# Down products of the first feed-forward chunks moved two units earlier and halved, one PSUM bank changed, residual additions given priority

## Chip, cores and metric

The kernel runs on one NeuronCore of a Trainium2 chip. The metric is the device time of one execution in microseconds (us): the median of three runs, 1444.62 us before the change (1444.34 to 1444.73). The engines are TensorE (PE, with its weight loads shown as PEld), VectorE (DVE), ScalarE (ACT), GpSimd (POOL) and SyncE (SP, which issues most DMAs).

## The reference

A decoder trunk of two layers works on 512 tokens of 1024 channels, in float32. Layer 0 has a mixer of a gated linear recurrence and pooling, layer 1 a Conformer convolution module. In both, a cross-attention into 256 memory tokens follows, and then the part that matters here, a gated MLP with a short convolution on its gate:

```
def conv_ffn(x, norm, w_up, dw_w, dw_b, w_down):
    h = rms_norm(x, norm) @ w_up                       # 1024 -> 2 * 3072
    g = causal_dwconv(h[..., :D_FF], dw_w, dw_b)       # width 3
    u = h[..., D_FF:]
    return (jax.nn.gelu(g) * u) @ w_down               # 3072 -> 1024
...
x = x + conv_ffn(...)                                  # at the end of each layer
```

## The kernel before

Channels lie on the 128 partitions and tokens along the free dimension; the residual is eight tiles `X[0]` to `X[7]` of 128 x 512. A float32 product is made of three matmuls (`mm3`, lines 186 to 188): every operand is split into a rounded high part (an ACT copy) and the rest, its low part (a DVE subtraction); high by high, high by low and low by high are added in PSUM.

**The feed-forward part** (`ffn`, once for each layer) has 24 chunks of 128 hidden channels, 0 to 23. Chunks 0 and 1, the plain pairs, are made in `opening()` with plain products. Chunks 2 to 23 are made by `unit(c)`, one after the other. A unit treats gate and value weights and the two halves of the tokens as a 2 x 2 block product with seven block products in place of eight. They are called, in the order of PE: s1 (into bank H), s2 (into F), a12 (into G), s3 (into F), then a11 of the next unit (`ahead`, into the next G), then s4 (into H) and a22 (into F). H is one half of the single bank of the pool `stat`; G and F come from the pool of five `mm` banks. In units 2 and 3 (`first` and `second`) a block product is twelve matmuls of 256 columns; from unit 4 on a product into G or F joins high and low part in one pass (line 791, eight matmuls: four of 512 columns and four of 256), and that into H stays twelve of 256.

**The weights of a unit** are four blocks, loaded by SP into `raw` (two blocks) and `wa` (two). The sums of blocks that the seven products need are made by DMAs that add in place, issued by POOL (lines 843, 846, 848), each after the split of the block that the addition overwrites. Each of the seven blocks is split by ACT (line 833) and DVE (line 840). The split of s1 and s2 for unit c+1 stands near the end of unit c.

**The gating of chunk c** begins at the end of unit c: DVE adds H and a copy of F (`add`, line 171), multiplies by the norm's scale, and then the convolution, the GeLU (line 918), the product with the value half (line 945) and the split of the result `ys[c]` (ACT line 948, DVE line 950) follow in small steps within unit c+1 (`next(left)`).

**The down products** of a group of four chunks are spread over the four units after it: unit c, for c from 4 on, takes 24 matmuls of 512 columns for two of the eight residual tiles (`Down`), into the two `aux` banks. In unit 4 (`seeded` is false) the banks start empty and DVE adds them to `X` (line 884). In later units ACT copies two `X` tiles into the banks first (`bank`, line 873) and copies them back after (`home`, line 878). The weights, 512 KB for each unit, come by one DMA into a `big` tile and are split by ACT (line 200) and DVE (line 203), one unit ahead; units 2 and 3 have no down products. The last group's products stand after the last unit; in layer 0 eight residual additions follow there (`sum`, line 884), each with `nxt.feed`: a square on ACT (line 251) and its addition on DVE (line 253). Their total gives the scale of the next norm (`norm.scale()`: line 319, then 355), and that the first product of the Conformer module. The weights of that module are split at the same time (line 167) with a priority of 100 instructions ahead (`AHEAD`).

**Order.** Within `opening` and the units the order of PE, ACT, DVE and POOL is the order of the program (`manual_schedule`); each of them takes its instructions strictly in that order. Outside, a scheduler orders them by priority; `high_priority(n)` moves an instruction n places ahead.

## Time and profile before

| | |
|---|---|
| median of three runs | 1444.62 us (1444.34 to 1444.73) |
| the profiled execution's own time | 1442.98 us |
| its span in the trace | 1441.2 us |
| busy PE, DVE, ACT, POOL | 1421.0, 1131.2, 939.2, 317.1 us |
| mean granted TensorE clock | 0.995 of full speed |

The views used are: the page of the whole profile; the waits, as a row "who waited <- for whom: us in total, times, longest"; the windows, one row for each stretch of time with the busy time of PE, PEld, DVE, ACT and POOL (instructions begun in brackets), the granted clock, the DMA engines' share and GB/s; the chain of waits, which is the work that ended last in order of time (start, us, what); and the timeline (start, us, engine, line, operation, out<-in, shape, count, and in square brackets the idle time before it and what ended it). Names such as `stat`, `mm`, `aux`, `raw` are tiles of the program. A matmul's duration in the timeline overlaps that of the next one, so what a block of matmuls takes is read from start to start. Units are counted from the start of their s1: in layer 0 unit 2 starts at 381.42, unit 3 at 391.50, unit 4 at 404.94 and unit 5 at 422.11 us of the span; in layer 1 at 1075.15, 1085.23, 1099.51 and 1117.57 us.

### The profile page before, as it was taken

Reading aid. Unit: us, or ns where it says so; the run is one execution under the profiler, and the core shown is the slowest. Engines: PE = TensorE matmul, PEld = TensorE weight load, DVE = VectorE, ACT = ScalarE, POOL = GpSimd, SP = SyncE. Lnnn points to the kernel's source line nnn. Section 1 sums busy time; section 2 is a strip of 40 time slices with the busy share of each in tenths; the row PEclk is TensorE's granted clock in tenths of the full one; section 3 lists DMA queues with packets and bytes.
Section 4 is the critical chain, followed back from the end, with each engine's and each line's share of the span. In section 5 each row is a group of like instructions: output and inputs, shape, how many; then the busy total and the mean of one; then the engine's idle time right before and its main releaser. Section 6 shows DMA issues by size and latency. Waiting matters only on the chain.

```text
span 1441.2 us, 22110 instructions
## 1 busy us (share of the span) xinstructions
PE 1421.0 (99%) x8142; PEld 1239.8 (86%) x8142; DVE 1131.2 (78%) x1908; ACT 939.2 (65%) x1704; POOL 317.1 (22%) x333
## 2 busy tenths in 40 slices
PE   9999999999999999999999999999998999999998
PEld 8888888988988888888878777899898888888887
DVE  6987776779777777777788997978787777777776
ACT  7568755667556676666665547767755676676664
POOL 0012300100112222122008992010002222222211
PEclk9999999999999999999999999999999999999999
DMA  8522232544477777776432354345337777777741
GB/s 304 190 87 90 88 131 68 124 109 139 100 173 174 165 178 169 165 183 161 142 117 88 118 165 142 110 85 135 110 96 176 166 172 175 167 174 171 174 127 59
DMA packets 80029, 204.28 MB, mean 142 GB/s; under 512 B 9008, under 2 KB 9520, under 8 KB 79920
## 3 DMA queue, kind: packets, MB, share of 16 engines
q1 hardware_dynamic: 50832, 150.15, 31.9%
q0 software_dynamic: 28800, 52.44, 21.2%
q8 instruction: 64, 1.05, 0.3%
q14 instruction: 45, 0.37, 0.1%
q10 hardware_dynamic: 288, 0.27, 0.1%
HBM read 145.16 MB, written 2.10 MB: 102 GB/s over the span
## 4 chain that ended last, share of the span: by engine, by line
PE 88%; DVE 4%; ACT 2%; POOL 2%; DMA 2%; issue 2%; SPq 0%; POOLq 0%; ACTq 0%; DVEq 0%
PE mm L791 19%; PE mm L187 12%; PE mm L186 12%; PE mm L188 12%; PE aux L186 7%; PE aux L187 7%; PE aux L188 7%; PE stat L186 3%; PE stat L188 3%; PE stat L187 3%; PE mm L463 2%; DMA raw<-wa 1%; DMA raw<-in_wv 1%; POOL actf L1550 1%; PE aux L538 0%
## 5 line engine op out<-in xcount | busy, mean ns | idle before, releaser
L186 PE MATMUL mm<-act,whi 128*128 128x512 f32 (+2 forms) x837 | 295.2, 354 | 1.7 <-ACT act L279 1.5
L187 PE MATMUL mm<-act,whi 128*128 128x512 f32 (+2 forms) x837 | 296.3, 354 | 0.3 <-DVE act L181 0.2
L188 PE MATMUL mm<-act,wlo 128*128 128x512 f32 (+2 forms) x837 | 295.8, 353 | 0.0
L791 PE MATMUL mm<-bigr,bigr 128*128 128x512 f32 x960 | 190.0, 341 | 0.0
L186 PEld LDWEIGHTS mm<-act,whi 128*128 128x128 f32 x837 | 158.1, 189 | 24.2 <-ACT act L279 2.0
L187 PEld LDWEIGHTS mm<-act,whi 128*128 128x128 f32 x837 | 158.5, 189 | 22.9 <-DVE act L167 1.0
L188 PEld LDWEIGHTS mm<-act,wlo 128*128 128x128 f32 x837 | 158.5, 189 | 21.0 <-DVE wlo L167 0.6
L840 DVE TENSOR_TENSOR bigr<-raw,bigr 128x512 fp32r<-128x512 f32 x176 | 121.0, 688 | 59.8 <-ACT bigr L833 56.0
L791 PEld LDWEIGHTS mm<-bigr,bigr 128*128 128x128 f32 x960 | 149.2, 190 | 18.3
L833 ACT ACTIVATE bigr<-raw 128x512 fp32r<-128x512 f32 x176 | 109.4, 624 | 75.8 <-DVE wlo L203 70.2
L846 POOL DMA_DIRECT2D raw<-wa x100 | 87.3, 893 | 310.7 <-DVE bigr L840 210.8
L186 PE MATMUL aux<-act,whi 128*128 128x512 f32 x399 | 155.6, 390 | 0.0
L187 PE MATMUL aux<-act,whi 128*128 128x512 f32 x399 | 155.5, 390 | 0.0
L188 PE MATMUL aux<-act,wlo 128*128 128x512 f32 x399 | 155.3, 389 | 0.0
L166 ACT ACTIVATE whi<-raw 128x1024 fp32r<-128x1024 f32 (+1 forms) x95 | 96.6, 1021 | 80.4 <-PE mm L187 44.4
L843 POOL DMA_DIRECT2D raw<-raw x50 | 43.3, 866 | 364.6 <-DVE wlo L840 281.1
L171 DVE TENSOR_TENSOR tmp<-mm,tmp 128x256 f32<-128x256 f32 x202 | 80.7, 418 | 51.7 <-ACT tmp L923 50.4
L791 PE MATMUL mm<-act,whi 128*128 128x512 f32 x320 | 119.4, 396 | 0.0
L923 ACT ACTIVATE tmp<-mm 128x256 f32<-128x256 f32 x160 | 55.5, 372 | 81.4 <-PE mm L791 81.4
L167 DVE TENSOR_TENSOR wlo<-raw,whi 128x1024 fp32r<-128x1024 f32 (+1 forms) x75 | 90.4, 1210 | 17.4 <-ACT whi L166 17.1
L188 PEld LDWEIGHTS aux<-act,wlo 128*128 128x128 f32 x399 | 74.9, 188 | 16.0
L187 PEld LDWEIGHTS aux<-act,whi 128*128 128x128 f32 x399 | 74.9, 188 | 15.9
(377 smaller groups left out, 3453.1 us busy)
## 6 DMA issues: line engine op xcount, KB each, us to landing
raw<-wa POOLq DMA_DIRECT2D x150, 256.0 KB, 3.4
wa<-in_wpair SPq DMA_DIRECT2D x88, 256.0 KB, 3.8
raw<-in_wpair SPq DMA_DIRECT2D x44, 512.0 KB, 3.7
big<-in_wdown SPq DMA_DIRECT2D x42, 512.0 KB, 4.5
raw<-raw POOLq DMA_DIRECT2D x50, 256.0 KB, 4.0
raw<-in_pw SPq DMA_DIRECT2D x24, 512.0 KB, 3.3
raw<-in_win SPq DMA_DIRECT2D x20, 512.0 KB, 3.3
raw<-in_wk SPq DMA_DIRECT2D x16, 512.0 KB, 3.3
```

What stands on the lines that cost most here:

```text
L166: A.activation(hi, src, AF.Copy)
L167: fetched[1] = (eng or V).tensor_tensor(lo, src, hi.bitcast(F32), op=ALU.subtract)
L171: V.tensor_tensor(out, a, b, op=ALU.add)
L186: PE.matmul(ps, wh, xh, start=first, stop=False, skip_group_check=onto)
L187: PE.matmul(ps, wh, xl, start=False, stop=False, skip_group_check=onto)
L188: return PE.matmul(ps, wl, xh, start=False, stop=last, skip_group_check=onto)
L791: PE.matmul(to, part, by, start=first and c == 0 and i == 0, stop=c == 3 and i == 1, skip_group_check=True)
L833: A.activation(self.w[name][0], self.block(name), AF.Copy)
L840: V.tensor_tensor(lo, self.block(name), hi.bitcast(F32), op=ALU.subtract)
L843: G.dma_start(self.r, self.z, accum_op=ALU.add)
L846: G.dma_start(block, self.a22, accum_op=ALU.add)
L923: A.activation(out, ps[:, M:], AF.Copy)
```

## The change

Four things are changed, the first three in both layers.

- The down products of chunks 0 to 3 no longer stand as 24 matmuls in each of the units 4 to 7. They are cut by chunk: chunks 0 and 1 go to units 2 and 3, two jobs of twelve matmuls in each (one job is two residual tiles), and chunks 2 and 3 to units 4 to 7, one job of twelve in each. The first job of a unit stands where the down products stood, behind s3; the second one stands between s4 and a22, and its copies home behind a22.
- The weights for that come as `Halves`: two DMAs of 256 KB into one `big` tile, which serves two jobs. They are loaded and split for unit 2 (split within unit 2), unit 3 (at the end of unit 2), units 4 and 5 together (at the end of unit 3) and units 6 and 7 together (in unit 5). From unit 8 on all is as before.
- H of units 2 and 3 is an `mm` bank in place of the `stat` bank.
- The eight residual additions at the end of layer 0's feed-forward part, with their squares, get the priority `URGENT` (600 places).

```
--- before.py
+++ after.py
@@ -856,15 +856,13 @@
         class Down:
 
 
-            def __init__(self, g, j):
-                self.g, self.j = g, j
-
-            def load(self):
-                self.w = Piece(I["wdown"][(layer * NG + self.g) * (C // 2) + self.j], big_f())
-
-            def products(self, i, ps, seeded=False, ks=range(GC)):
-                for k in ks:
-                    self.last = mm3(ps, blk(self.w, k * 2 * P + i * P), ys[self.g * GC + k], k == 0 and not seeded, k == GC - 1, seeded)
+            def __init__(self, g, j, ks, at=0):
+                self.g, self.j, self.ks, self.at = g, j, ks, at
+
+            def products(self, i, ps, seeded=False, ks=None):
+                for k in self.ks if ks is None else ks:
+                    at = self.at + (k - self.ks[0]) * 2 * P + i * P
+                    self.last = mm3(ps, blk(self.w, at), ys[k], k == self.ks[0] and not seeded, k == self.ks[-1], seeded)
 
             def bank(self, i, seeded):
 
@@ -885,7 +883,41 @@
                 if self.g == NG - 1:
                     nxt.feed(n)
 
-        downs = {c: Down(*divmod(c - GC, GC)) for c in range(GC, CF + GC)}
+        class Halves(Piece):
+
+
+            def __init__(self, js, half):
+                self.raw = big_f()
+                for i, j in enumerate(js):
+                    src = I["wdown"][layer * NG * (C // 2) + j]
+                    nc.sync.dma_start(self.raw[:, i * T : (i + 1) * T], src[:, half * T : (half + 1) * T])
+
+        group = [list(range(g * GC, (g + 1) * GC)) for g in range(NG)]
+        old, new = group[0][:2], group[0][2:]
+        downs = {c: [Down(*divmod(c - GC, GC), group[c // GC - 1])] for c in range(2 * GC, CF + GC)}
+        halves = {}
+        for i, c in enumerate((PLAIN, PLAIN + 1)):
+            downs[c] = [Down(0, 2 * i + k, old, k * T) for k in range(2)]
+            halves[c] = (2 * i, 2 * i + 1), 0
+            for k in range(2):
+                downs[GC + 2 * i + k] = [Down(0, 2 * i + k, new, k * T)]
+            halves[GC + 2 * i] = (2 * i, 2 * i + 1), 1
+        for c in (GC + 1, GC + 3):
+            halves[c] = None
+
+        def fetch_down(c):
+
+            if c <= CF and halves.get(c, 0) is not None:
+                d = downs[c][0]
+                w = Halves(*halves[c]) if c in halves else Piece(I["wdown"][(layer * NG + d.g) * (C // 2) + d.j], big_f())
+                for d in downs[c] + (downs[c + 1] if halves.get(c + 1, 0) is None else []):
+                    d.w = w
+
+        def split_down(c):
+            if c <= CF and halves.get(c, 0) is not None:
+                downs[c][0].w.high()
+                downs[c][0].w.low()
+
         done = set()
 
         def high(c, name):
@@ -970,8 +1002,26 @@
 
             nonlocal left, chains
             G, F = chains
-            down, seeded = downs.get(c), c > GC
-            H = stat_ps()[:, :M]
+            jobs = iter(downs[c])
+            H = main_ps()[:, :M] if c <= second else stat_ps()[:, :M]
+
+            def seeds():
+                nonlocal down, d, seeded
+                down, seeded = next(jobs, None), seeded is not None or c > first
+                if down:
+                    d = [down.bank(i, seeded) for i in range(2)]
+
+            def products():
+                if down:
+                    for ks in (down.ks[:-1], down.ks[-1:]):
+                        for i in range(2):
+                            down.products(i, d[i], seeded, ks)
+
+            def home(i):
+                if down:
+                    down.home(i, d[i], seeded)
+
+            down, d, seeded = None, None, None
             m(c, H, "s1", seven.T1)
             if c <= second:
                 high(c + 1, "s3")
@@ -987,8 +1037,9 @@
                 A.activation(u[:, :M], F, AF.Copy)
             if c == first:
                 both(c + 2, "a11")
-            if down:
-                d = [down.bank(i, seeded) for i in range(2)]
+                split_down(c)
+                fetch_down(c + 1)
+            seeds()
             next(left, None)
             both(c + 1, "s3")
             next(left, None)
@@ -1020,36 +1071,37 @@
             both(c + 2, "a11")
             high(c + 1, "a12")
             low(c + 1, "a12")
-            if down:
-                for ks in (range(GC - 1), (GC - 1,)):
-                    for i in range(2):
-                        down.products(i, d[i], seeded, ks)
+            products()
             if c + 3 in pairs:
                 pairs[c + 3].load()
             if c + 2 in pairs and c > first:
                 pairs[c + 2].load_second()
-            if c > second and c + 1 in downs:
-                downs[c + 1].w.high()
-                downs[c + 1].w.low()
-            if c + 2 in downs and first < c <= CF - 2:
-                downs[c + 2].load()
+            if c > second:
+                split_down(c + 1)
+                fetch_down(c + 2)
             high(c + 1, "s1")
             low(c + 1, "s1")
             high(c + 1, "s2")
             low(c + 1, "s2")
-            if c == second:
-                downs[c + 1].w.high()
-                downs[c + 1].w.low()
-            if down:
-                down.home(0, d[0], seeded)
+            if c <= second:
+                split_down(c + 1)
+                fetch_down(c + 2)
+            home(0)
 
             if c + 1 in pairs:
                 chains = ahead(c + 1)
-            if down:
-                down.home(1, d[1], seeded)
+            home(1)
+            more = len(downs[c]) > 1
+            if more:
+                seeds()
 
             m(c, H, "s4", seven.B22, False)
+            if more:
+                products()
             m(c, F, "a22", seven.T4, False)
+            if more:
+                home(0)
+                home(1)
             left = gating(c, g, f, u, F, H)
             next(left)
 
@@ -1107,7 +1159,7 @@
             w[-1].low()
             pairs[second + 1].load()
             pairs[second + 1].load_second()
-            downs[GC].load()
+            fetch_down(first)
             t = seven.sums(3, lambda: (next(g), next(g)))
             next(t)
             next(g, None)
@@ -1158,17 +1210,18 @@
             parked = []
             for n in range(PARKED):
                 if n + 1 < C // 2:
-                    downs[CF + n + 1].w = load_w(I["wdown"][(layer * NG + NG - 1) * (C // 2) + n + 1])
+                    downs[CF + n + 1][0].w = load_w(I["wdown"][(layer * NG + NG - 1) * (C // 2) + n + 1])
                 parked.append(mem.key_piece(n, park=True))
             for j in range(C // 2):
                 for i in range(2):
                     ps = mm_ps()
-                    downs[CF + j].products(i, ps)
-                    downs[CF + j].sum(i, ps)
-            mem.behind = downs[CF + C // 2 - 1].last.ins
+                    downs[CF + j][0].products(i, ps)
+                    with tc.high_priority(URGENT):
+                        downs[CF + j][0].sum(i, ps)
+            mem.behind = downs[CF + C // 2 - 1][0].last.ins
             return mem, parked
         else:
-            finish([ys[(NG - 1) * GC + k] for k in range(GC)], downs[CF].w)
+            finish([ys[(NG - 1) * GC + k] for k in range(GC)], downs[CF][0].w)
 
     def finish(y, w):
```

## Prediction

> **What bounds the kernel now.** I read the page first, then the waits of TensorE, then windows around the places that those name, then the chain of waits and the timeline of ACT and DVE there.
>
> ```profile
> span 1441.2 us, 22110 instructions
> PE 1421.0 (99%) x8142; PEld 1239.8 (86%) x8142; DVE 1131.2 (78%) x1908; ACT 939.2 (65%) x1704; POOL 317.1 (22%) x333
> ```
>
> TensorE is the bound nearly everywhere: 1421.0 of 1441.2 us. The change takes no matmul away, so it can win only where PE idles or runs at a lower clock. The waits of PE say where:
>
> ```profile
> PE stat L186 <- DVE tmp L171: 6.9, 2, 3.8
> PE mm L186 <- ACT act L279: 1.5, 1, 1.5
> ```
>
> The first row is two waits, one in each layer: the s1 product of unit 4 waits for the `stat` bank until DVE has added unit 3's H. The second is the start of the Conformer. The windows of units 2 to 5 (four rows for each layer), and of that start, give their full price:
>
> ```profile
> core 0: us, PE busy (x) PEld busy (x) DVE busy (x) ACT busy (x) POOL busy (x), PEclk, DMA share, GB/s
> 381.42:391.50 10.08, 10.08 (x86) 10.08 (x85) 7.24 (x14) 5.18 (x11) 2.24 (x3) 1.00 0.53 111
> 391.50:404.94 13.44, 10.43 (x83) 10.03 (x82) 10.38 (x18) 7.81 (x14) 3.85 (x6) 1.00 0.87 214
> 404.94:422.11 17.17, 17.17 (x90) 15.18 (x91) 12.74 (x22) 8.21 (x16) 4.28 (x5) 0.90 0.64 155
> 422.11:437.47 15.36, 15.36 (x90) 13.55 (x89) 11.80 (x20) 10.37 (x20) 2.54 (x4) 1.00 0.69 169
> 1085.23:1099.51 14.28, 10.43 (x83) 10.03 (x82) 10.38 (x18) 7.83 (x14) 4.44 (x6) 0.95 0.86 210
> 1099.51:1117.57 18.06, 18.06 (x89) 15.96 (x90) 12.76 (x22) 8.20 (x16) 3.55 (x5) 0.85 0.63 149
> 742.40:750.00 7.60, 4.86 (x15) 3.23 (x14) 6.93 (x13) 3.12 (x5) 0.00 (x0) 0.78 0.00 0
> ```
>
> Unit 2 takes 10.08 us with PE always busy (1.44 us for each of seven products). Unit 3 has 10.43 us of work and takes 13.44 (layer 1: 14.28): 3.01 and 3.85 us idle. Unit 4 should take unit 5's 15.36 and 0.23 for one more matmul (row below), 15.59; it takes 17.17 and 18.06, at a granted clock of 0.90 and 0.85: 1.58 and 2.47 us lost. Both layers together lose **10.9 us**. At the Conformer's start PE idles 7.60 - 4.86 = 2.74 us, and the clock of 0.78 costs 7.60 x 0.22 = 1.67.
>
> The chain of waits shows what held DVE before unit 4, and, in its last rows, the matmuls of units 4 and 5:
>
> ```profile
> 394.80 6.72 DMA raw<-wa
> 401.63 0.63 ACT bigr L833
> 402.26 0.95 ACT whi L200
> 403.24 1.23 DVE wlo L203
> 404.46 0.34 DVE tmp L171
> ...
> 419.19 0.23 PE mm L962
> ...
> 423.71 4.22 PE mm L791 x24
> ...
> 433.38 1.41 PE mm L791 x8
> ```
>
> An adding DMA needs 6.72 us while the DMA engines are 87% busy (window of unit 3); the split of s2 waits for it, and DVE's addition of H stands behind that split. Down products between 427.94 and 433.38 are 24 matmuls in 5.44 us, so twelve are **2.72 us**, and a joined product is 1.41 us.
>
> **The change, part by part.** *Units 2 and 3 get 24 matmuls each.* The same 96 matmuls a layer run, so this is 5.44 us longer for each of these units and 2.72 us shorter for units 4 to 7: zero. With 10.88 us more before unit 4, and its s1 in a bank that units 2 and 3 no longer use, neither the late DMA nor the `stat` bank is waited for there. I take the whole 10.9 us as saved.
>
> *Units 4 to 7 become shorter than DVE's own round.* PE needs 15.36 - 2.72 = 12.64 us now (12.87 in unit 4, with the matmul of line 962). But s1 of the next unit still waits for DVE's addition of H, and what stands before that addition needs PE only until s2. In unit 5 (start 422.11):
>
> ```profile
> 425.15 0.39 ACT L923 ACTIVATE tmp<-mm 128x256 f32<-128x256 f32 x1 [1.98 <-PE mm L791]
> 425.43 1.12 ACT L873 ACTIVATE aux<-x 128x512 f32<-128x512 f32 x2
> 426.99 0.62 ACT L833 ACTIVATE bigr<-raw 128x512 fp32r<-128x512 f32 x1
> 428.97 0.63 ACT L948 ACTIVATE act<-tmp 128x512 fp32r<-128x512 f32 x1 [0.84 <-DVE tmp L945]
> 427.64 0.69 DVE L840 TENSOR_TENSOR bigr<-raw,bigr 128x512 fp32r<-128x512 f32 x1 [1.51 <-ACT bigr L833]
> 429.64 0.69 DVE L950 TENSOR_TENSOR act<-tmp,act 128x512 fp32r<-128x512 f32 x1 [0.70 <-ACT act L948]
> 433.78 1.22 DVE L203 TENSOR_TENSOR wlo<-big,whi 128x1024 fp32r<-128x1024 f32 x1
> 434.91 1.47 DVE L840 TENSOR_TENSOR bigr<-raw,bigr 128x512 fp32r<-128x512 f32 x2
> 436.30 0.42 DVE L171 TENSOR_TENSOR tmp<-stat,tmp 128x256 f32<-128x256 f32 x1
> ```
>
> ACT copies F at 3.04 us after the unit's start, then seeds, GeLU, the split of s3; DVE starts on s3 at 5.53, waits 0.70 for `ys`, and works without a gap from 7.53 to the addition of H, which ends at 14.61. With 0.14 us from there to PE (404.46 + 0.34 to 404.94) the next unit cannot start before 14.75. Today 15.36 of matmuls hide that, by 0.61. After the change unit 7, which splits unit 8's weights as today, takes 14.75: a wait of 2.11. Unit 5 also splits, but fetches nothing for unit 7, so s2's split need not wait for a `big` buffer (some 0.19 less, an estimate: the two splits of 434.91 take 1.39 to the next row, where two of 0.69 that overlap a little would take 1.20): 14.56, a wait of 1.92. Units 4 and 6 split no down weights: 433.78 to 434.91 falls away, 14.56 - 1.13 = 13.43; in unit 6 a wait of 0.79. Unit 4 meets something later first: its job is only chunks 2 and 3, and chunk 3's `ys` is finished by L948 and L950, at 7.49 and 8.22 us. Today 18 matmuls stand before chunk 3's; now it is six. PE begins the job behind one product of 1.44 and three of 1.41, at 5.67, comes to chunk 3 at 5.67 + 1.36 = 7.03, and waits there for the high part until 7.5 and one matmul (0.23) later for the low part until 8.25; the five matmuls left end at 9.42 in place of 8.39: 1.03 us. Unit 4 takes 13.90. **Sum 5.85 us for a layer.**
>
> *The second job of units 2 and 3 waits for its banks.* Both `aux` banks must be emptied first.
>
> ```profile
> 387.80 0.42 DVE L171 TENSOR_TENSOR tmp<-stat,tmp 128x256 f32<-128x256 f32 x1 [0.46 <-ACT tmp L1011]
> 390.61 0.42 DVE L171 TENSOR_TENSOR tmp<-stat,tmp 128x256 f32<-128x256 f32 x1
> 419.68 1.28 DVE L884 TENSOR_TENSOR x<-x,aux 128x512 f32<-128x512 f32 x2
> 398.61 0.62 ACT L833 ACTIVATE bigr<-raw 128x512 fp32r<-128x512 f32 x1
> 435.57 0.58 ACT L878 ACTIVATE x<-aux 128x512 f32<-128x512 f32 x1
> ```
>
> In unit 2 DVE is free of its splits at 390.61 - 381.42 = 9.19. Two splits of down weights come before (1.13 each; 0.46 of the first fits into the idle time ahead of 387.80): 10.99. The first residual addition ends 0.68 later, at 11.67, and a seed of 0.56 makes the bank ready at 12.3. PE is there after six products and one job, 6 x 1.44 + 2.72 = 11.36: a wait of 0.9. In unit 3 the queue is ACT's. The split of s1 ends at 399.23 - 391.50 = 7.73 today; two seeds before it (1.04), then s2 (0.52), the down split (0.95), copy home, F and home again (0.50 each) and the first seed (0.56) make 12.3 (start to start, an estimate from the rows above) against PE's 11.56: 0.7. These are bounded by zero (if the splits come earlier) and about 2 us each (if the adding DMA for s2 is as late as today); I take **1.6 us a layer**. The eight more seeds and eight more copies home (8 x 0.52 + 8 x 0.49 = 8.1 us of ACT) are otherwise hidden: ACT works 5.18 and 7.81 us in units that now take 15. The bytes are the same; four more DMA issues a layer stand on SP, whose loads go out a unit ahead.
>
> *Residual additions first.* What decides the Conformer's start:
>
> ```profile
> 734.24 1.22 DVE L167 TENSOR_TENSOR wlo<-raw,whi 128x1024 fp32r<-128x1024 f32 x1
> 737.51 1.28 DVE L884 TENSOR_TENSOR x<-x,mm 128x512 f32<-128x512 f32 x2
> 739.04 1.48 DVE L253 TENSOR_TENSOR tmp<-tmp,tmp 128x512 f32<-128x512 f32 x2
> 734.34 0.28 PE L186 MATMUL mm<-bigr,act 128*128 128x256 f32 x1
> 742.29 0.28 PE L188 MATMUL mm<-bigr,act 128*128 128x256 f32 x1
> 746.14 0.54 PE L186 MATMUL mm<-act,whi 128*128 128x512 f32 x1 [1.50 <-ACT act L279]
> ```
>
> The last down product is done where the memory keys begin, 734.34, but its addition is late, behind weight splits such as that of 734.24; the total of squares is there at 740.52. With priority: addition 735.1, square 735.75, total 736.5, so 4.0 us earlier. A displaced split of 1.13 may fall into the chain's gaps; I give back 0.6. The first product comes at 742.7 in place of 746.14, PE has keys until 742.41, 0.3 us stays idle and the clock need not fall: 2.74 + 1.67 - 0.3 = **4.1 us** saved, and at worst none.
>
> *Sum against the profiled execution* (1442.98 us; the median of the runs lies 1.64 higher): - 10.9 + 2 x (5.85 + 1.6) - 4.1 = - 0.1. That is 1442.9, as a median **1444.5**: no change that can be measured (0.2%, 2.9 us, is about what a measurement can tell).
>
> **Rivals.** *The clock falls in the new waits* (slower). The gate is in the rows: after 3.01 us idle the clock was 0.90 over 17.17 us, which is 1.72 us lost. The waits of 1.92 and 2.11 us at units 5 and 7 are shorter, yet at the Conformer's start 2.74 us of idle, in pieces, was enough. Two drops give + 3.4, 1447.9; four give 1451.4. The Trainium skill, "TensorE: Matmul & The Clock Gate", section "Part 1: The HAM clock gate", says that the clock halves only after a whole idle window of about 3.4 us. By that rule the new waits would cost nothing beyond themselves, but the wait of 3.01 us would not have either, and the trace shows that it did; no run here shows where between 2.1 and 3.0 us the point lies.
>
> *The priority moves nothing* (slower): ACT and DVE still have the splits to do, the scheduler fills the chain's gaps with them, and the total of squares stays at 740. DVE works 6.93 of 7.60 us there, which speaks for it; that it idles while the scale is spread speaks against. 1444.5 + 4.1 = 1448.6.
>
> *The small waits are covered* (faster): seeds and chunk 3's `ys` come early enough in units 2 to 4. The ordered queues speak against it. 2 x (1.6 + 1.03) = 5.3 less: 1439.2.
>
> *DVE's round does not decide* in units 5 to 7, because its queue runs ahead of what the steady unit shows. Then 2 x 4.82 = 9.6 less: 1434.9. The unbroken row of DVE from 7.53 to 14.61 speaks against it.
>
> **How the numbers follow.** Forecast, 1441.6 to 1447.4: 0.42. Clock: 0.13. Priority moves nothing: 0.16. Small waits covered: 0.15. DVE's round does not decide: 0.08. Something else, to either side: 0.06. Faster is 0.15 + 0.08 + 0.03 = 0.26, slower 0.13 + 0.16 + 0.03 = 0.32. The range, 1439.0 to 1449.5, leaves out the last faster case, four drops of the clock and half of the rest.
>
> **What would show it.** The waits of PE should lose the two of 3.0 and 3.8 us and gain `stat` after DVE L171 six times, of 1.9, 0.8 and 2.1 us; an `aux` product of unit 4 should wait for L948 or L950 by about 1 us, and one in units 2 and 3 for the seeds (ACT on `aux`). The starts of s1 should lie 16.4, 16.6, 13.9, 14.6, 13.4 and 14.75 us apart from unit 2 on, and the total of squares near 736.5 less than 2.5 us behind the last down product. The prediction is wrong if units 5 to 7 take 12.7 us, if they show a clock under 1.00, or if the first product behind the total of squares is as late as today.

## The result, and the profile after

The changed kernel takes 1447.94 us (median of twelve runs, 1445.71 to 1450.03) against 1444.33 us (1441.56 to 1446.05) for the kernel before beside it. The ratio is 1.0027 with an interval of 1.0018 to 1.0036: 3.6 us or 0.25% slower, where no change was forecast. The profiled execution took 1448.33 us, 5.35 us more than that of before. The profiled before lay 1.35 us under its median and the profiled after 0.39 us over its own, so the traces show 1.74 us more than the medians do.

The head of the page after. The busy time of PE, DVE and POOL is the same within 1.2 us, ACT has 15.1 us more (the seeds and copies home, forecast as 16.2), and the span is 5.3 us longer:

```profile
span 1446.5 us, 22163 instructions
PE 1422.0 (98%) x8142; PEld 1235.9 (85%) x8142; DVE 1130.0 (78%) x1908; ACT 954.3 (66%) x1736; POOL 316.7 (22%) x333
```

The waits of PE after (who <- for whom: us in total, times, longest). In the new code the seeds' copies are line 871 and the split of `ys` lines 980 and 982; line 791 is the one-pass product as before.

```profile
PE stat L186 <- DVE tmp L171: 5.7, 6, 1.4
PE aux L186 <- ACT aux L871: 2.9, 4, 1.0
...
PE mm L791 <- DVE tmp L171: 1.4, 6, 0.2
...
PE aux L186 <- ACT act L980: 0.8, 2, 0.4
...
PE aux L187 <- DVE act L982: 0.4, 2, 0.2
```

The two waits of 3.0 and 3.8 us are gone. In each layer two waits on the same bank, of 1.26 to 1.41 us at s1 of units 6 and 8, two for the seeds and a pair for chunk 3's `ys` stand in their place, as forecast. The third wait on `stat` that was forecast for each layer, 0.8 us at unit 7, is listed with 0.14 and 0.16 us only; that the first row says six is no confirmation, since small waits at other places are among them. The row of `mm` after L171 was not forecast: products into G or F that wait for DVE to read a bank. The windows of units 2 to 9 of layer 0, and of the stretch from the last down product to the Conformer's first product (same columns as before; H of unit 3 is no longer in `stat`, so the border between units 2 and 3 is set by eye and only their sum, 33.50, is used):

```profile
core 0: us, PE busy (x) PEld busy (x) DVE busy (x) ACT busy (x) POOL busy (x), PEclk, DMA share, GB/s
381.33:398.05 16.72, 15.75 (x109) 14.33 (x108) 10.71 (x18) 9.93 (x18) 3.46 (x4) 1.00 0.74 176
398.05:414.83 16.78, 16.26 (x109) 14.82 (x108) 10.41 (x18) 12.04 (x23) 3.44 (x4) 1.00 0.45 108
414.83:428.88 14.05, 13.45 (x79) 11.38 (x78) 9.97 (x18) 8.47 (x18) 2.21 (x3) 1.00 0.68 163
428.88:443.45 14.57, 13.04 (x78) 11.16 (x76) 11.13 (x20) 10.28 (x20) 3.17 (x5) 1.00 0.69 151
443.45:456.96 13.51, 13.12 (x77) 11.22 (x77) 10.57 (x20) 9.34 (x19) 3.43 (x5) 1.00 0.75 180
456.96:471.60 14.64, 13.14 (x76) 11.21 (x77) 11.71 (x21) 10.40 (x20) 3.44 (x5) 1.00 0.80 192
471.60:487.53 15.93, 15.69 (x89) 13.57 (x90) 12.47 (x21) 10.43 (x21) 4.11 (x5) 1.00 0.72 168
487.53:502.87 15.34, 15.34 (x89) 13.55 (x88) 11.80 (x20) 10.36 (x20) 3.37 (x4) 1.00 0.76 172
738.35:749.24 10.89, 8.94 (x71) 8.39 (x70) 9.70 (x17) 6.64 (x11) 0.00 (x0) 1.00 0.72 229
```

Units 4 to 8 take 14.05, 14.57, 13.51, 14.64 and 15.93 us, and layer 1 the same within 0.02. The clock is at 1.00 in all of them. How much each place loses, from the starts of units and the forecast's own times for the work (10.08 + 10.43 + 2 x 5.44 for units 2 and 3, 12.87, three times 12.64, 15.36):

| place, each layer | forecast us | measured us |
|---|---|---|
| units 2 and 3, second job's banks | 1.60 | 2.11 |
| unit 4, chunk 3's `ys` | 1.03 | 1.18 |
| unit 5, DVE's round | 1.92 | 1.93 |
| unit 6, DVE's round | 0.79 | 0.87 |
| unit 7, DVE's round | 2.11 | 2.00 |
| unit 8 | 0 | 0.57 |
| sum | 7.45 | 8.66 |

Before lost 10.9 us there in both layers together; after loses 17.3. That is 6.4 us more, where the forecast had 4.0. The last place, the Conformer's start, gave much less than forecast. From the first memory-key product behind the last down product (734.34 before, 738.35 after) the total of squares ends after 6.17 us before and 3.45 after, and the first Conformer product starts after 11.80 and 10.89: **0.9 us gained**, where the forecast had 3.4 for this start. The rest of its 4.1 us was the clock, which should have stayed up behind the start. In these two traces it was at half for one stretch of 3.41 us before and after alike, so nothing was gained there (a window of before, then one of after):

```profile
746.45:749.86 3.41, 3.23 (x10) 2.54 (x10) 3.41 (x6) 2.01 (x4) 0.00 (x0) 0.50 0.00 0
749.58:752.99 3.41, 3.21 (x10) 2.54 (x10) 3.41 (x6) 2.01 (x4) 0.00 (x0) 0.50 0.06 24
```

6.4 - 0.9 is 5.5 us, and the spans differ by 5.3.

DVE's queue there shows why (timeline after; the last residual addition is line 882, the last addition of squares 741.11):

```profile
738.77 0.68 DVE L882 TENSOR_TENSOR x<-x,mm 128x512 f32<-128x512 f32 x1
739.37 0.68 DVE L167 TENSOR_TENSOR act<-raw,act 128x512 fp32r<-128x512 f32 x1
739.97 1.22 DVE L167 TENSOR_TENSOR wlo<-raw,whi 128x1024 fp32r<-128x1024 f32 x1
741.11 0.69 DVE L253 TENSOR_TENSOR tmp<-tmp,tmp 128x512 f32<-128x512 f32 x1
...
742.95 1.23 DVE L167 TENSOR_TENSOR wlo<-raw,whi 128x1024 fp32r<-128x1024 f32 x1 [0.52 <-ACT whi L166]
744.09 0.17 DVE L327 RECIPROCAL rtok<-rtok 128x4 f32<-128x4 f32 x1
...
744.50 0.69 DVE L332 SCALAR_TENSOR_TENSOR act<-ident,rhi 128x512 fp32r<-128x512 f32 x1
...
745.36 1.23 DVE L167 TENSOR_TENSOR wlo<-raw,whi 128x1024 fp32r<-128x1024 f32 x1
746.50 0.69 DVE L332 SCALAR_TENSOR_TENSOR act<-ident,rlo 128x512 fp32r<-128x512 f32 x1
```

The residual additions did go ahead of the weight splits. But the splits that they passed are now in the next parts of the same chain, three of 1.2 us: one before the last addition of squares, one before the reciprocal, and one between the two diagonals that spread the scale. The last square and the square root stand on ACT:

```profile
739.55 0.64 ACT L251 ACTIVATE tmp<-x 128x512 f32<-128x512 f32 x1
...
743.04 0.26 ACT L326 ACTIVATE rtok<-stat,eps 128x4 f32<-128x4 f32 x1
```

The square is done at 740.19 and its addition starts at 741.11, 0.9 us later; the root is done at 743.30 and the reciprocal starts at 744.09, 0.8 us later. The chain from the total of squares to the first product has grown from 5.6 to 7.4 us.

The place that was not in the forecast, unit 8, is one delay handed on. DVE's timeline after (`tmp<-stat` is the addition of H that frees `stat` for unit 8, `tmp<-mm` at 475.85 the last read of bank F before s3; the two rows from 486.31 are the same pair for unit 9):

```profile
471.04 0.42 DVE L171 TENSOR_TENSOR tmp<-stat,tmp 128x256 f32<-128x256 f32 x1
...
475.85 0.42 DVE L171 TENSOR_TENSOR tmp<-mm,tmp 128x256 f32<-128x256 f32 x1
...
486.31 0.42 DVE L171 TENSOR_TENSOR tmp<-stat,tmp 128x256 f32<-128x256 f32 x1 [0.36 <-PE stat L188]
...
491.13 0.42 DVE L171 TENSOR_TENSOR tmp<-mm,tmp 128x256 f32<-128x256 f32 x1
```

The read of F ends 5.2 us after the addition of H begins, in both units. In unit 9 the addition lies 1.22 us before the unit's start, and the read is over 4.02 us into the unit, before PE asks for s3. In unit 8 it lies only 0.56 us before the start, because PE was waiting for it; the read is over 4.67 us into the unit, and s3 waits:

```profile
471.60 0.35 PE L186 MATMUL stat<-bigr,bigr 128*128 128x256 f32 x1 [1.26 <-DVE tmp L171]
...
476.32 1.68 PE L791 MATMUL mm<-bigr,bigr 128*128 128x512 f32 x8 [0.24 <-DVE tmp L171]
```

Unit 8 has all 15.36 us of PE work, so nothing hides this. Idle times in brackets are smaller than what a place loses, because the last matmul ahead of a wait is listed with its whole duration (0.39 us for 512 columns at 428.46 in before, where the next one starts 0.23 us later); the unit spacing is the better measure.

### The profile page after: what moved, and what is told of

Same layout as the page of the kernel before. It is cut to its first block, busy times and chain, and to the rows that moved or that the text cites. A ratio compares the mean times of both kernels' runs of the same rounds, so it can differ in the third digit from the quotient of the medians.

```text
span 1446.5 us, 22163 instructions
## 1 busy us (share of the span) xinstructions
PE 1422.0 (98%) x8142; PEld 1235.9 (85%) x8142; DVE 1130.0 (78%) x1908; ACT 954.3 (66%) x1736; POOL 316.7 (22%) x333
## 4 chain that ended last, share of the span: by engine, by line
PE 82%; DVE 7%; ACT 6%; issue 2%; POOL 2%; DMA 1%; SPq 0%; POOLq 0%; DVEq 0%; ACTq 0%
PE mm L791 16%; PE mm L187 12%; PE mm L186 12%; PE mm L188 12%; PE aux L186 6%; PE aux L187 6%; PE aux L188 6%; PE stat L186 2%; PE stat L188 2%; PE stat L187 2%; PE mm L463 2%; DVE bigr L840 1%; ACT bigr L833 1%; ACT aux L871 1%; DMA raw<-in_wv 1%
## 5 line engine op out<-in xcount | busy, mean ns | idle before, releaser
L171 DVE TENSOR_TENSOR tmp<-mm,tmp 128x256 f32<-128x256 f32 x210 | 84.0, 419 | 48.8 <-ACT tmp L955 47.7
L186 PEld LDWEIGHTS aux<-act,whi 128*128 128x128 f32 x399 | 74.9, 188 | 19.2 <-ACT aux L871 3.8
L187 PEld LDWEIGHTS aux<-act,whi 128*128 128x128 f32 x399 | 74.9, 188 | 16.6 <-DVE act L982 1.1
```

Source lines behind the costliest of these rows:

```text
L171: V.tensor_tensor(out, a, b, op=ALU.add)
L186: PE.matmul(ps, wh, xh, start=first, stop=False, skip_group_check=onto)
L187: PE.matmul(ps, wh, xl, start=False, stop=False, skip_group_check=onto)
```

## The experiments

The theory for the result: the moved products cost about 6 us net, new waits of 17.3 us against before's own 10.9, most of them DVE's round in units 5 to 7, and the priority gains only a part of 4 us because the passed splits fill the chain behind the squares. The rivals: the moved products alone cost nothing net and something else is slower; the clock decides; the freed `stat` bank decides; the priority is worth nothing. Ratios are to the kernel before, run beside each, whose medians were 1443.71 to 1443.77 us.

### after_noprio: the changed kernel without the priority

```diff
-                    with tc.high_priority(URGENT):
-                        downs[CF + j][0].sum(i, ps)
+                    downs[CF + j][0].sum(i, ps)
```

> The kernel after without the priority. Theory A: the feed-forward part carries all the loss, the priority gives about 0.9 us; so this is 0.9 us slower than after, 1448.8, ratio to before 1.003 to 1.004. Theory B (the priority is worth 4.1 us and something else in the tail costs 3): ratio 1.005 to 1.006.

Measured: 1450.17 us (1449.08 to 1450.59), ratio 1.0041 (1.0028 to 1.0053). The moved products and the bank change by themselves cost 5.9 us (4.0 to 7.7); the forecast's own terms for them gave 4.0. In this trace the total of squares ended 6.34 us behind the first key product, and the first Conformer product started 11.95 behind it, as before. Against the changed kernel's 1.0027, the priority is worth roughly 2 us there, not 4.1. The trace of that one execution shows where more than the 1.06 us of the start can come from: behind the start the clock is at half for 6.83 us, from 749.40, where the changed kernel has 3.41.

### prio_only: the kernel before with the priority

```diff
-                    downs[CF + j].sum(i, ps)
+                    with tc.high_priority(URGENT):
+                        downs[CF + j].sum(i, ps)
```

> The kernel before with one part of the change: the residual additions at the end of layer 0 have priority. Theory A (the weight splits that they displace fill the gaps of the scale's chain): first product of the Conformer 0.9 us earlier behind the last down product, as in the trace of after; ratio 0.999 to 1.000. Theory B (my prediction; what was seen in after is spoilt by the units ahead of it): 4.1 us less, ratio 0.997.

Measured: 1441.71 us (1439.60 to 1442.69), ratio 0.9982 (0.9973 to 0.9991), a gain of 2.6 us (1.3 to 3.9). The total of squares ended after 3.44 us, the first product started after 10.98 (11.80 before), and the clock was at half for 3.41 us behind it: the same picture as in the changed kernel. The forecast's 4.1 lies outside this interval, and so does nothing. The profiled executions differ by 3.4 us, but 2.7 of that lie in units 3 and 4 (13.47 and 15.65 us in layer 0, 14.07 and 17.03 in layer 1), which this edit does not touch: their stall cost 8.2 us in this execution, where the forecast had read 10.9. Two executions alone can't price the priority.

### tail_fix: two of four weight splits held back behind the chain

The priority as in the last one, and of the Conformer's four weights that were split early only two; the other two are split once the norm's last copy is issued, and the two loads behind them are issued after that too.

```diff
-        for _ in range(4):
+        for n in range(4):
             fetch()
-            weights()
-        fetch()
-        fetch()
+            if n < 2:
+                weights()
...
+        with tc.issue_after(norm.copied[7]):
+            weights()
+            weights()
+        fetch()
+        fetch()
```

> The kernel before with the priority of the residual additions, and the splits of two of the four weights that filled the gaps of the scale's chain held back behind its last copy. Theory A (those splits ate the priority's gain): from the last down product to the first product of the Conformer 9 us or less, where before has 11.80 and after 10.89, the clock does not fall there, and the time is 2 to 4 us under that of the priority alone: 1438 to 1440, ratio 0.996 to 0.998. Theory B (the chain itself has that length, the splits stand only beside it): 10.5 to 11 us, ratio 0.998 to 0.9995.

Measured: 1439.09 us (1437.97 to 1441.93), ratio 0.9968 (0.9957 to 0.9980): 2.0 us better than the priority alone by the ratios, 2.6 by the medians. DVE's timeline of the same chain (the total of squares is 737.32, the first product starts at 743.54):

```profile
737.32 0.68 DVE L253 TENSOR_TENSOR tmp<-tmp,tmp 128x512 f32<-128x512 f32 x1
...
739.54 0.18 DVE L327 RECIPROCAL rtok<-rtok 128x4 f32<-128x4 f32 x1 [0.92 <-ACT rtok L326]
...
739.96 0.69 DVE L332 SCALAR_TENSOR_TENSOR act<-ident,rhi 128x512 fp32r<-128x512 f32 x1
...
740.76 0.69 DVE L332 SCALAR_TENSOR_TENSOR act<-ident,rlo 128x512 fp32r<-128x512 f32 x1
```

From the total of squares to the second diagonal it is 3.44 us in place of 5.39 (741.11 to 746.50). The first product starts 8.99 us behind the first key product (10.98 with the priority alone, 11.80 before), the clock does not fall there, and the first sigmoid behind it comes at 21.67 in place of before's 25.63: 4.0 us. Of these 4.0 us, 2.8 are the earlier start, and the other 1.2 come behind it, where the clock now stays up. So the gain that I forecast for the tail exists, but it needs the splits kept out of the chain, which the change does not do.

### after_tail: the changed kernel with the same two splits held back

The edit of `tail_fix`'s second part, on the changed kernel.

```diff
-            weights()
-        fetch()
-        fetch()
+            if n < 2:
+                weights()
...
+        with tc.issue_after(norm.copied[7]):
+            weights()
+            weights()
+        fetch()
+        fetch()
```

> The kernel after with the splits of two of the four weights held back behind the scale's chain. Theory A (tail and feed-forward part are independent): the tail gives 2 to 4 us as it did on the kernel before, 1444 to 1446, ratio to before 1.000 to 1.001, so that the moved products alone cost what the tail gains. Theory B (the tail's gain belongs to the old order of units): under 1 us gained, ratio 1.0025.

Measured: 1444.83 us (1444.05 to 1446.45), ratio 1.0007 (0.9998 to 1.0016). The first product again starts after 8.99 us and the sigmoid after 21.67. It is some 3 us less than the changed kernel: with the tail as forecast, the whole change comes out where the forecast had put it, at no change.

### h_only: only the bank of H moved, in the kernel before

```diff
-            H = stat_ps()[:, :M]
+            H = main_ps()[:, :M] if c <= second else stat_ps()[:, :M]
```

> The kernel before with one part of the change: H of units 2 and 3 in an mm bank; the down products stay in units 4 to 7. Theory A (DVE's round sets the pace only where PE has less than 14.75 us a unit; the lag of about 3 us that DVE has at the end of unit 3 is worked off by the slack of 0.6 us of each later unit): unit 4's s1 starts at once, the waits of 3.0 and 3.8 us and both falls of the clock go, waits of 0.5 us or less are left in units 4 and 5. That is 8 to 10 us less than before: 1434 to 1436, ratio 0.993 to 0.995. Theory B (the lag only moves): a wait of 2 to 3 us shows in unit 4's s3 or at unit 5's s1, and the time is within 3 us of before, ratio 0.998 to 1.000.

Measured: 1439.11 us (1438.55 to 1439.68), ratio 0.9966 (0.9954 to 0.9979): 4.7 us faster with one line. The waits for `stat` are gone, and smaller ones have come one or two products later, at s2 and s3 of unit 4 (waits of PE):

```profile
PE mm L791 <- ACT mm L963: 2.2, 2, 1.8
...
PE mm L791 <- DVE tmp L171: 1.2, 1, 1.2
```

The result lies between the two theories: the bank was somewhat under half of the 10.9 us. The rest I put down to the late DMA and to ACT's and DVE's queues behind it, which is not shown: `late_s2` below, which attacks them by order, gains hardly more. Unit 4 still loses 2.2 us in layer 0 and 3.6 in layer 1 (17.77 and 19.18 against 15.59), unit 5 0.4 in each.

### after_stat: the changed kernel with H of units 2 and 3 back in `stat`

```diff
-            H = main_ps()[:, :M] if c <= second else stat_ps()[:, :M]
+            H = stat_ps()[:, :M]
```

> The kernel after with one part undone: H of units 2 and 3 is in the stat bank again. Theory A (with the products in units 2 and 3 DVE has added H long before the next s1): no wait for stat at units 3 and 4, the same time as after within 1 us. Theory B (the bank is what removed the wait of before): waits of 1 us or more at s1 of units 3 and 4, 2 us or more a layer slower than after.

Measured: 1448.19 us (1447.65 to 1449.10), ratio 1.0031 (1.0020 to 1.0041), the same as the changed kernel. Units 2 and 3 take 16.88 and 16.55 us, unit 4 14.03. With 24 matmuls more in each of these units the bank is free in time anyway: once the products are moved, the bank change does nothing. Either edit alone takes away the wait for the bank, and one of them costs one line, though `h_only` still loses 2.2 and 3.6 us at unit 4.

### extra_dve: one more split for DVE in units 4 to 7

A low part is computed a second time (0.7 us of DVE, the same values); nothing else is touched.

```diff
+            if GC <= c < 2 * GC:
+                pairs[c + 1].low("a12")
             products()
```

> The kernel after with the split of a12's low part done twice in units 4 to 7: one more DVE operation of 128x512, 0.60 us from start to start, ahead of the addition of H. Theory A (DVE's round sets the length of units 5 to 7): units 5, 6, 7 are 0.6 us longer, 15.2, 14.1 and 15.2 us, unit 4 between 0 and 0.6, unit 8 up to 0.6; some 2.2 us a layer, 4.4 in all, so 1452.3, ratio to before 1.005 to 1.006. Theory B (the adding DMAs or the mm banks set it, DVE only stands beside): no unit changes by more than 0.2 us, 1448.

Measured: 1455.48 us (1453.32 to 1457.67), ratio 1.0078 (1.0064 to 1.0092), 7.5 us over the changed kernel. Windows of units 5 to 8:

```profile
429.18:444.55 15.37, 13.15 (x77) 11.24 (x77) 12.40 (x22) 10.27 (x20) 3.65 (x5) 1.00 0.66 142
444.55:460.30 15.75, 14.63 (x76) 12.65 (x77) 11.35 (x21) 9.33 (x19) 3.44 (x5) 0.89 0.68 163
460.30:475.67 15.37, 13.11 (x76) 11.24 (x77) 12.40 (x22) 10.40 (x20) 3.44 (x5) 1.00 0.73 175
475.67:492.59 16.92, 16.92 (x89) 15.02 (x90) 12.46 (x21) 10.39 (x20) 4.05 (x5) 0.90 0.66 156
```

Units 5 and 7 grow by 0.80 and 0.73 us, the size of one split, with the clock at 1.00: DVE's round sets them. Unit 4 grows only by 0.12, so DVE's round does not set that one. Units 6 and 8 grow by 2.2 and 1.0 for another reason too: their first product has waited 2.0 us, and the clock is granted at half for 3.4 us behind each of these waits.

### free_matmuls: eight more matmuls in units 5 and 7

They write a used bank, and nothing reads the result.

```diff
             m(c, F, "a22", seven.T4, False)
+            if c in (GC + 1, GC + 3):
+                for _ in range(8):
+                    PE.matmul(d[0], ones, seven.block(seven.T1, 0), start=True, stop=True, skip_group_check=True)
```

> The kernel after with eight more matmuls of 512 columns, 1.82 us, behind a22 in units 5 and 7 of each layer; they write to an emptied aux bank and nobody reads them. Theory A (DVE's round sets these units, PE has 1.9 to 2.1 us to spare): units 5 and 7 stay at 14.6 us, the four additions cost under 0.5 us together, ratio to after 1.000 (to before 1.0025). Theory B (PE or its banks set them): each costs 1.8 us, 7.3 in all, ratio to before 1.0075.

Measured: 1448.13 us (1446.66 to 1449.13), ratio 1.0027 (1.0018 to 1.0036), as the changed kernel. 32 matmuls of 0.23 us, 7.3 us of PE work, cost nothing. The wait moves into them (waits of PE):

```profile
PE stat L186 <- DVE tmp L171: 0.8, 4, 0.3
```

Units 5 and 7 take 0.27 and 0.48 us more (14.84, 15.12) and unit 8 takes 0.47 less (15.46): with more work on PE, DVE's addition of H lies earlier against the unit's start and the wait of s3 is smaller. That shows the hand-on of unit 8 from its other side. PE in units 5 and 7 is not the bound after the change; the products were taken out of units that could not get shorter.

### after_order: the two queue waits attacked by order

Unit 4's job is put behind s4, and the next down weights' split behind the second job's seeds.

```diff
-            products()
+            if c != GC:
+                products()
...
-            if c <= second:
-                split_down(c + 1)
-                fetch_down(c + 2)
...
             if more:
                 seeds()
+            if c <= second:
+                split_down(c + 1)
+                fetch_down(c + 2)
+            more = more or c == GC
```

> The kernel after with another order in units 2 to 4: the split of the next down weights behind the seeds of the second job in units 2 and 3, and unit 4's job behind s4. Theory A (my steps for these three waits): the waits of 1.24 and 0.79 us for the seeds fall under 0.2, that for chunk 3 in unit 4 is gone and unit 4 becomes 13.4 to 13.5 us in place of 14.05; units 5 to 8 stay at 14.6, 13.5, 14.6 and 15.9. Some 2.6 us a layer, 5 in all: 1442.5 to 1443.5, ratio 0.9985 to 1.000 to before. Theory B (these waits only move on to the next product): 1447, ratio 1.002.

Measured: 1450.03 us (1449.30 to 1451.57), ratio 1.0045 (1.0032 to 1.0057): some 2 us worse than the changed kernel. The seeds of unit 2 are no longer waited for, and those of unit 3 for 0.24 us in each layer. But the job no longer stands in front of s4, and s4 now waits 2.64 us in each layer for DVE to read H. The job had been the cover of that read. In layer 0 the clock falls behind that wait as well. The forecast had priced the waits one by one; here one wait's cure uncovers the next.

### late_s2: the stall of before, attacked without moving products

`h_only`, and in unit 3 s2's split, which waits for the adding DMA, goes behind the first step of the gating of chunk 3; a11 of unit 4 is issued ahead of it.

```diff
             if c == second:
-                downs[c + 1].w.high()
-                downs[c + 1].w.low()
+                chains = ahead(c + 1)
+            else:
+                high(c + 1, "s2")
+                low(c + 1, "s2")
...
             next(left)
+            if c == second:
+                high(c + 1, "s2")
+                low(c + 1, "s2")
+                downs[c + 1].w.high()
+                downs[c + 1].w.low()
```

> H of units 2 and 3 in an mm bank as in the last such kernel, down products in units 4 to 7 as before, and in unit 3 alone what waits for the late adding DMA goes last: the split of s2 for unit 4 and that of its down weights stand behind the first step of the gating, and the a11 product of unit 4 with its copy of G to F stands ahead of them. Theory A (the whole loss before unit 4 is DVE and ACT standing in order behind that one DMA): the waits of 1.2 and 1.8 us that the last kernel kept (s3 of unit 4 for DVE, s2 for ACT's copy to F) fall under 0.5 us, no fall of the clock before unit 5, and the time is 9 to 11 us under before, 1433 to 1435, ratio 0.9925 to 0.994. Theory B (the DMA is late for s2 in any order): s2 of unit 4 waits 1 to 2 us, ratio 0.996.

Measured: 1438.52 us (1437.80 to 1440.78), ratio 0.9967 (0.9955 to 0.9980), hardly more than `h_only`; the 9 to 11 us of the first theory did not come. Unit 4 takes 17.93 and unit 5 15.79 us. The wait has split up (timeline of PE at s2 and s3 of unit 4):

```profile
403.72 0.50 PE L791 MATMUL mm<-bigr,bigr 128*128 128x512 f32 x1 [0.56 <-ACT bigr L833]
404.44 1.44 PE L791 MATMUL mm<-bigr,bigr 128*128 128x256 f32 x7 [0.22 <-DVE bigr L840]
...
408.04 1.20 PE L791 MATMUL mm<-bigr,bigr 128*128 128x512 f32 x5 [0.75 <-DVE tmp L171]
```

Now s2's split itself is the last to come, and then DVE is late for s3. The clock no longer falls at unit 4 in either layer, but 2.3 us of lag are left at unit 4 and 0.4 at unit 5.

### best_tail: late_s2 and tail_fix together, no product moved

```diff
+            H = main_ps()[:, :M] if c <= second else stat_ps()[:, :M]
...
             if c == second:
+                chains = ahead(c + 1)
...
+                    with tc.high_priority(URGENT):
+                        downs[CF + j].sum(i, ps)
...
+            if n < 2:
+                weights()
```

> The first and the second kernel of this group together, without any of the moved products. Theory A: the gains add, 11 to 14 us under before, 1430 to 1433, ratio 0.990 to 0.9925. Theory B (either one shifts the other's wait): no better than the better one of the two.

Measured: 1433.53 us (1433.10 to 1434.04), ratio 0.9930 (0.9917 to 0.9942): 10.2 us faster than before, a little short of the 11 expected, and about 14 faster than the changed kernel. The gains of the two parts (5.3 and 4.7 us) add. The clock stays at full speed from 6.1 us to 1429.5 us of the span. The version keeps the down products where they were.

## Why the prediction was wrong

**The step that failed most: "A displaced split of 1.13 may fall into the chain's gaps; I give back 0.6."** There were three such splits of 1.2 us each, and all fell into the chain: the one ahead of the last addition of squares held it up by 0.9 us, the one ahead of the reciprocal by 0.8, the one between the diagonals by 1.2 (2.00 us from diagonal to diagonal, 0.80 in `tail_fix`). That is 2.9 us in place of 0.6. The total of squares came 2.7 us earlier in place of 4.0, and the first product 0.9 in place of about 3.4. The prediction's own sign of being wrong came with it: from the total of squares to the first product it is 7.4 us, later even than before's 5.6. And with PE still idle there, the other term of the 4.1 us, 1.67 for a clock that "need not fall", was not saved either: in the changed kernel it is at half for the same 3.41 us as before. `tail_fix` holds two of the splits back (and two loads behind them), and then the first product comes 2.8 us earlier and the clock does not fall; `after_tail` does it in the changed kernel and wins some 3. This is mostly the mechanism of my rival "the priority moves nothing" (the scheduler fills the gaps with splits), except that the total of squares did move; its time, 1448.6, is close to what was measured, but in part for another reason, below. I had read DVE's 6.93 busy of 7.60 us as a sign for that rival and yet costed the forecast with one split. Two of the splits stood in the trace of before right there, at 734.24 and 736.37; an addition that passes them does not take them out of DVE's queue.

**A second, smaller failure: the sum of the new waits, "5.85 us for a layer" and "1.6 us a layer".** They measured 8.66 together in place of 7.45. 0.57 is unit 8, where no wait was listed: I followed DVE's round to the addition of H and stopped there, though s3 needs the next thing in the same queue, the read of F, and a queue that is late for one is late for the other. 0.5 is the second jobs' banks in units 2 and 3, whose estimate lay near the middle of its bounds; 0.15 is chunk 3's `ys`. That is 2.4 us in both layers.

**What held.** DVE's round in units 5, 6 and 7 was forecast as 14.56, 13.43 and 14.75 us, and took 14.57, 13.51 and 14.64: the row of DVE's work without a gap up to the addition of H was the right thing to read, and `extra_dve` and `free_matmuls` show that it sets these units and PE does not. The waits of before are gone, the whole 10.9 us of that trace. How much they are worth on average is less certain than the forecast took it: the same units lose 8.2 us in the trace of `prio_only` and 11.1 in that of `tail_fix`. Chunk 3's `ys` holds unit 4. The clock stayed at 1.00 in the new waits, so that rival did not occur; but `extra_dve` shows that some 0.6 us more of wait brought it about in both layers. The rival "DVE's round does not decide" is refuted by the same two, "small waits covered" by the 2.11 and 1.18 us of the table.

By the timed runs the two parts are +5.9 us (`after_noprio`) and about -2 us (the priority on top), some +4 together, against +4.0 and -4.1 forecast: each failure is worth about 2 us. By the traces they are 3.2 us (tail) and 2.4 (waits). One reason for the difference in the tail: behind the Conformer's start the clock is at half for 3.41 us in each of the six traces that have the priority and hold no split back (`after`, `prio_only`, `after_stat`, `after_order`, `extra_dve`, `free_matmuls`) and in before, for 6.83 us in the three others without the priority (`after_noprio`, `h_only`, `late_s2`), and not at all in the three with the splits held back; 3.41 us at half are 1.7 us lost, so before's trace shows the cheaper case. This is one execution of each kernel, so it is likely, not shown. The ratios of `after_noprio` and `prio_only` carry intervals of some 1.3 to 1.9 us to each side. That the priority gives less than 4.1 us lies outside its interval; that the new waits cost more than 4.0 does not, since 4.0 us is the low end of the interval of `after_noprio`, and rests on the traces.

The change as such spends its main part on the wrong resource. Of the 12 matmuls' time taken out of each unit from 5 to 7, units 5 and 7 keep 0.8 and 0.7 us of 2.72, since DVE cannot follow; the same 2.72 us are paid in full in units 2 and 3. The stall that the moved products remove was nearly in half a matter of one bank, as `h_only` shows. Why `late_s2` still loses 2.3 us at unit 4 was not taken further.

## What to carry to other kernels

Before work is moved out of a unit, find the shortest time that each other in-order engine needs from its first to its last hand-over in that unit: work taken out below that time saves nothing there and is still paid in full where it goes, and a unit that starts on a late engine also pays at the next thing that this engine hands over. When an operation gets priority over others in a latency chain, follow the others: they land in the chain's next gaps at full length unless they are made to wait for the end of the chain. A stall made of two causes, a bank and a late queue, should be tried with the cheap cause alone first.

## What the runs showed of the hardware that was not expected

**The clock falls after shorter waits than the forecast had, and not each time.** In `extra_dve` it fell to half for 3.4 us behind waits of 1.99 and 2.02 us, in both layers, at 0.89 and 0.90 over the windows shown. The changed kernel's waits at the same places, 1.40 and 1.26 us, did not bring it down in either layer. In `after_order` a wait of 2.64 us stands in unit 4 of each layer, from 421.1 and from 1119.9 us on; it cost the clock in layer 0 and nothing in layer 1. What differs is where the wait lies. Before the end of this trace the clock changes at 425.03, 428.44, 752.71 and 756.12 us, which are 1, 95 and 1 times 3.413 us apart. Laid out in steps of that length, the time around the two waits is this:

```profile
421.62:425.03 3.41, 1.27 (x11) 1.30 (x11) 3.38 (x8) 3.17 (x8) 0.00 (x0) 1.00 0.83 199
425.03:428.44 3.41, 3.41 (x12) 2.73 (x11) 2.61 (x5) 0.00 (x0) 1.72 (x2) 0.50 0.76 180
1117.94:1121.35 3.41, 1.93 (x11) 1.31 (x9) 2.70 (x5) 2.57 (x6) 0.86 (x1) 1.00 0.32 56
1121.35:1124.76 3.41, 2.25 (x16) 2.15 (x17) 3.38 (x8) 2.19 (x5) 0.75 (x1) 1.00 0.71 193
```

In layer 0 one step has most of the wait, PE is busy for 1.27 us of its 3.41, and the next step runs at half (0.50, 1.7 us lost). In layer 1 the wait is shared by two steps, PE is busy for 1.93 and 2.25 us in them, and the clock stays. The 13 traces, laid out in the same way, agree: each step at full clock with PE busy for less than 1.66 us is followed by one at half, and of the 21 falls ahead of the kernels' ends 20 follow a step with at most 1.69 us (the other one, 2.35 us, at the Conformer's start in `after_noprio`). So it is not the length of a wait that counts, but whether PE is busy for less than about half of one such step; that "half" is an estimate from these rows.

The Trainium skill, "TensorE: Matmul & The Clock Gate", section "Part 1: The HAM clock gate", says that the activity window runs freely, so that a warm-up varies with where in the window it begins: the steps of these traces agree with that, for the fall too. Its figure for the fall, one idle window of about 3.4 us, does not agree with the falls behind 2.0 us; here the measurement decides.

**Idle time in several pieces can leave the clock alone.** `h_only` loses 3.6 us at unit 4 of layer 1, with one wait of 1.79 us and a fall of the clock, and 2.2 us in layer 0, with two waits of 0.39 and 1.23 us and no fall. `late_s2` loses 2.3 us in each layer, in three waits of 0.56, 0.22 and 0.75 us (layer 0), and the clock stays up in both.
